# Placing the split of the last stage's weights, and the final norm's second broadcast, in a hybrid diffusion trunk layer

## The chip, the cores and the metric

The kernel runs on one core of one Trainium2 chip, written at the level of single engine instructions. The metric is the device time of one execution in microseconds; before the change the median of three runs is 3129.58 us (3123.66 to 3132.76).

TensorE multiplies, VectorE, ScalarE and GpSimd work element by element, and SyncE's queue issues all the DMAs that matter here. All matrix work is done in a split form: an fp32 operand x becomes a rounded part h (`wih`, `wph`, `hh`, ...) and the rest l = x - h (`wil`, `wpl`, `hl`, ...), and one product is three passes, h by h, h by l and l by h. ScalarE makes h (`hi`), VectorE makes l (`lo`).

## The reference

One trunk layer is evaluated for 2048 latent and 256 context tokens with shared weights (D_MODEL 1024, four branches of width 512):

```
h = rmsnorm(x) * (1 + scale) + shift
u = h @ w_in                                   # 8960 columns, split among the branches
o_att, o_conv, o_pool, o_ssm = the four mixers of the columns of u
br = [o_att*silu(g_att), o_conv*silu(g_conv), o_pool*silu(g_pool), o_ssm*silu(g_ssm)]
proj = einsum('blnw,nwd->blnd', br, w_br)      # each branch to 1024
merged = sum over branches of sigmoid(g_mrg) * proj
y = rmsnorm(x + gate * (merged @ w_out)) * final_g
```

The attention is a softmax over a band of latent keys, the context keys and a sink. The convolution has 31 taps per channel and a layer norm behind it. The scan branch ends in a product with `glu_w`. So `glu_w`, `w_br` and `w_out` are first needed near the end, and `w_in` all through.

## The kernel before

**Stages.** The tokens are six chunks of 384 columns, in three groups of 768. The first stage (to about 1065 us) makes the modulation, the normed h and the scan, with input columns of `w_in` beside it. The second (to about 2346 us) computes the other input columns, ten planner steps to each, while convolution, pooling and attention run in the background. The third takes each group through `glu_group` (the scan branch's last product), `merge_group` (32 products with `w_br`), `out_group` (8 products with `w_out`) and `last_norm`.

**Who orders the work.** `flow` writes out TensorE's order. It holds one dense stream (the columns) and a list of background streams, all of them Python generators. A generator yields what it waits for: tiles, a time of the planner's clock (a float), or a condition. The class `Clock` estimates when each tile is ready, and `flow` takes a background stream as soon as it is ready by that clock, and the dense stream otherwise; if nothing is ready it moves the clock forward. The order so found is binding for TensorE alone (`manual_schedule(engines={PE})`). On ScalarE, VectorE, GpSimd and SyncE a scheduler with a cost model of its own orders the instructions by when it believes their inputs and buffers to be ready; it may put an instruction before others that the program issued earlier. On the chip each of these engines takes its instructions in the order so fixed.

**The pieces.** `presplits` is a background stream of the second stage. It splits `glu_w`, `w_br` and `w_out` in 112 pieces of [128, 2, 128], with a load into a raw buffer `wps`, `hi` into `wph` on ScalarE, `lo` into `wpl` on VectorE and a store of each into a scratch tensor in HBM (`wd_glu`, `wd_br`, `wd_out`), from which the third stage fetches whole tiles. Piece n may be issued once `self.steps >= n * rate` with `rate = 0.9 * self.total / 112`, where `total` is the number of column steps of the stage. There are three buffers `wps`, with loads two pieces ahead, and one `wph` and one `wpl`.

**The tie.** `queue(eng, ins)` adds an ordering without a semaphore: `ins` may not be put before the instruction that was issued last on that engine when `self.behind` was taken. Before the change only the convolution's taps use it. `clock.last` holds each engine's latest instruction.

**The maxima.** `att_max` computes scores `mw` into PSUM, and VectorE adds the mask and takes the row maximum in one instruction (`tensor_tensor_reduce`), whose elementwise result goes into a scratch tile `junk` that nobody reads.

**The final norm.** `out_group` ends with `self.norms += 1` and hands `last_norm` over as a background stream. `last_norm` adds up the squares on TensorE (`st`), forms the reciprocal root, and then for each of two chunks m: VectorE builds a diagonal `dg`, TensorE broadcasts it with a product by ones into `rb` (one PSUM bank), VectorE multiplies eight tiles of the result with it, and they are stored. Between `dg` and the broadcast the stream holds for 4 us of the planner's clock in the first two groups (`g < 2`). At the end `self.norms -= 1`. The next group's `merge_group` computes its first column and then yields `(lambda: not self.norms,)`, and issues nothing more until that is true.

Of the kernel before, what the change touches and what calls it, by code (L numbers as in the profile page):

```python
# [12 lines left out]
F32 = mybir.dt.float32  # L13
F32R = mybir.dt.float32r
# [7 lines left out]
CH = 384  # L22
# [12 lines left out]
def f32(ap):  # L35
    return ap.bitcast(F32)
# [151 lines left out]
class K:  # L188
# [75 lines left out]
        return self.nc.sync.dma_start(out, in_)  # L264

    def hi(self, out, in_, scale=1.0):
        self.nc.scalar.activation(out, in_, AF.Copy, scale=scale)

    def lo(self, out, in_, hi, scale=None, eng=None):
        eng = eng or self.nc.vector  # L270
        if scale is None:
            eng.tensor_tensor(out, in_, f32(hi), op=OP.subtract)
        else:
            eng.scalar_tensor_tensor(out, in_, scale, f32(hi), op0=OP.mult, op1=OP.subtract)

    def rsqrt(self, pool, v, n, eng=None):
        V = eng or self.nc.vector
# [97 lines left out]
    def presplits(self, keys, pool):  # L375

        parts = [(key, k) for key in keys for k in range(0, self.WSRC[key[0]][1], 2)]
        rate = 0.9 * self.total / len(parts)
        got, to = [], {}

        def fetch(key, k):
            x = pool.tile([128, 2, 128], F32, name="wps", tag="wps", bufs=3)
            src = self.A[self.WSRC[key[0]][0]][key[1:] if len(key) > 2 else key[1]]
            self.load(x, src[:, k:k + 2])
            got.append(x)

        for p in parts[:2]:
            fetch(*p)
        for n, (key, k) in enumerate(parts):
            yield (lambda n=n: self.steps >= n * rate,)  # L390
            if n + 2 < len(parts):
                fetch(*parts[n + 2])
            kt = self.WSRC[key[0]][1]
            if k == 0:
                to[key] = self.dp.tile([2, 128, kt, 128], F32, name="wd_" + "_".join(str(x) for x in key))
            x = got.pop(0)
            h = pool.tile([128, 2, 128], F32R, name="wph", tag="wph", bufs=1)
            l = pool.tile([128, 2, 128], F32R, name="wpl", tag="wpl", bufs=1)
            self.hi(h, x)
            self.lo(l, x, h)  # L400
            for i, x in enumerate((h, l)):
                self.store(to[key][i][:, k:k + 2], f32(x))
            if k + 2 == kt:
                self.wcache[key] = to[key]
# [371 lines left out]
    def conv_setup(self, cp):  # L776
        nc, A = self.nc, self.A
        self.cw = cp.tile([128, 4, 31], F32, name="cw")
        self.cvec = cp.tile([128, 4, 4], F32, name="cvecs")
        self.load(self.cw, A["conv_dw"])  # L780
        self.load(self.cvec, A["conv_vec"])
        nc.vector.tensor_scalar(self.cw, self.cw, 0.5, None, op0=OP.mult)
        self.cgb = cp.tile([128, 4, 2], F32, name="cgb")
        nc.vector.tensor_scalar(self.cgb, self.cvec[:, :, 1:3], 0.5, None, op0=OP.mult)
        o5 = cp.tile([128, 128], F32R, name="o512")
        nc.vector.tensor_scalar(o5, self.ones, 1.0 / 512, None, op0=OP.mult)
        self.o512 = o5
        self.pwh = cp.tile([128, 4, 128], F32R, name="pwh")
        self.pwl = cp.tile([128, 4, 128], F32R, name="pwl")
        for k in range(0, 4, 2):  # L790
            x = cp.tile([128, 2, 128], F32, name="pw", tag="wps", bufs=3)
            self.load(x, A["pool_w"][:, k:k + 2])
            self.hi(self.pwh[:, k:k + 2], x)
            self.lo(self.pwl[:, k:k + 2], x, self.pwh[:, k:k + 2])
        self.pvec = cp.tile([128, 4], F32, name="pvec")
        self.load(self.pvec, A["pool_scale"])
        self.pfix = cp.tile([128, 4, 16], F32, name="pfix")
        self.load(self.pfix, A["pool_fix"])
# [34 lines left out]
    def queue(self, eng, ins):  # L833

        last = self.behind.get(eng)
        if last is not None:
            self.tc.add_manual_dep(ins.ins, last.ins.name, mybir.DependencyInfo(mybir.DependencyClass.NoSync,
                                                                               mybir.DependencyReason.DATA),
                                   reason="taps")

    def conv_taps(self, gc, mp, taps):

# [218 lines left out]
    def att_max(self, b, kv, t0, ka, kb, v, ap, st):  # L1061
# [32 lines left out]
        if wn:  # L1094
            for h in range(4):
                ps = self.px("mw", "m")[:, :wn]
                yield ps, ka
                nc.tensor.matmul(ps, qa[:, h, :], ka[:, w0:w0 + wn], start=True, stop=True)
                junk = ap.tile([128, CH], F32, name="junk", tag="junk", bufs=1)
                nc.vector.tensor_tensor_reduce(out=junk[:, :wn], in0=ps, in1=self.mask[:, moff:moff + wn], scale=1.0,  # L1100
                                               scalar=mc[:, h:h + 1], op0=OP.add, op1=OP.max,
                                               accum_out=mf[:, h:h + 1])

# [546 lines left out]
    def last_norm(self, g, y, S, mp, chunks):  # L1650

        nc = self.nc
        n = 3 * len(chunks)
        c0 = 3 * chunks[0]
        st = self.px("st", "x")
        Sf = S.rearrange("p c t -> p (c t)")
        yield Sf[:, c0 * 128:(c0 + n) * 128], st
        for i in range(n):
            nc.tensor.matmul(st[:, 2 * i:2 * i + 2], Sf[:, (c0 + i) * 128:(c0 + i + 1) * 128], self.ones[:, 0:2],
                             start=True, stop=True)  # L1660
        v = mp.tile([128, 6], F32, name="rms_v", tag="rms_v", bufs=2)
        nc.vector.tensor_scalar(v[:, :n], st[:, 0:2 * n].rearrange("p (i w) -> p i w", w=2)[:, :, 0], 1.0 / 1024, 1e-6,
                                op0=OP.mult, op1=OP.add)
        r = self.rsqrt(mp, v[:, :n], n, nc.gpsimd if g < 2 else None)
        sh = [128, 3, 128]
        for m, c in enumerate(chunks):
            dg = mp.tile(sh, F32, name="dg", tag="dg", bufs=1)
            nc.vector.tensor_tensor(dg, self.ident[:, None, :].to_broadcast(sh),
                                    r[:, 3 * m:3 * m + 3, None].to_broadcast(sh), op=OP.mult)
            rb = self.px("rb", "x")  # L1670
            yield dg, rb
            yield (self.clock.t + (4.0 if g < 2 else 0.0),)
            nc.tensor.matmul(rb[:, :CH], self.ones, dg.rearrange("p i q -> p (i q)"), start=True, stop=True)
            for d in range(8):
                yy = y[d][:, c * CH:(c + 1) * CH]
                nc.vector.scalar_tensor_tensor(yy, yy, self.fg[:, d:d + 1], rb[:, :CH], op0=OP.mult, op1=OP.mult)
                self.store(self.O["yT"][2 * g + c][:, d], yy)
        self.norms -= 1
# [302 lines left out]
```

## Time and profile before

| what | value |
|---|---|
| median of 3 runs | 3129.58 us (3123.66 to 3132.76) |
| profiled execution | 3132.41 us, its span 3130.7 us |
| TensorE matmuls | 2957.9 us, 94% of the span |
| VectorE | 2020.9 us, 65% |
| ScalarE | 1035.9 us, 33% |
| GpSimd | 874.4 us, 28% |
| mean granted clock of TensorE | 0.976 |
| DMA | 711.17 MB, mean 227 GB/s |

The profile records one execution. Busy times are per engine and may overlap; the granted clock is the share of full speed that TensorE was given, and 1.0 is 2.4 GHz. A matmul's end is modelled, so a busy share tells that TensorE had work, not that it ran at its peak. Nearly every instruction goes through one helper line (L162), so the rows are told apart by their tiles: `mm` is a bank of column products, `pj` of branch products, `tg`, `sg`, `mge`, `px`, `qf` are evictions of columns.

### The profile page before, as it was taken

To read this page: it belongs to the slowest core of one execution; us is meant where nothing else is said; L and a number is where in the kernel's file an instruction comes from. 1 tells how busy PE (TensorE), PEld (TensorE's weight loads), DVE (VectorE), ACT (ScalarE), POOL (GpSimd) and SP (SyncE) were. 2 spreads that over 40 slices of the span, in tenths; PEclk is the share of its full clock that TensorE was granted. 3 is DMA by queue.
4 is the path that set the end of the run, shared out by engine and by line. 5 is a ranking of instruction groups with operands and counts; after the bars stand their busy time and mean duration, and the time that the engine had idled before them with its cause. 6 is when DMAs were issued, how large, how long until landed. Compare 5 with 4: busy or idle time off the path is not lost.

```text
span 3130.7 us, 46156 instructions
## 1 busy us (share of the span) xinstructions
PE 2957.9 (94%) x16316; PEld 2823.2 (90%) x16316; DVE 2020.9 (65%) x3525; ACT 1035.9 (33%) x2029; POOL 874.4 (28%) x1124
## 2 busy tenths in 40 slices
PE   8979998999999998989999999999999999999998
PEld 4978898999899997989888889999999999999998
DVE  6835787767687476778787677777313653653663
ACT  5522333332332243335454444454312011011011
POOL 0953352434343131442232333233100001001001
PEclk9989999999999998999999999999999999999999
DMA  9665556565665688887767656575578976976967
GB/s 365 205 220 207 211 184 216 196 224 196 241 223 174 196 279 277 266 245 209 225 205 225 199 152 173 166 243 154 159 222 283 321 227 226 340 247 222 327 198 243
DMA packets 379904, 711.17 MB, mean 227 GB/s; under 512 B 83513, under 2 KB 207257, under 8 KB 378393
## 3 DMA queue, kind: packets, MB, share of 16 engines
q1 hardware_dynamic: 379672, 708.22, 68.9%
q8 instruction: 129, 2.11, 0.3%
q14 instruction: 103, 0.84, 0.1%
HBM read 470.43 MB, written 229.83 MB: 224 GB/s over the span
## 4 chain that ended last, share of the span: by engine, by line
PE 37%; DMA 7%; DVE 5%; issue 1%; ACT 1%; SPq 1%; DVEq 0%; ACTq 0%
PE mm L162 20%; PE pj L162 12%; PE ov L162 2%; DVE acc L162 2%; PE sT L162 1%; DMA bs<-sg_d 1%; DMA wbh<-wd_br 1%; DMA wd_out<-wpl 1%; DMA wd_out<-wph 1%; SPq L162 1%; DMA wil<-wd_out 1%; DMA bo<-o_d 0%; PE mw L162 0%; DVE wpl L162 0%; DVE pl L162 0%
## 5 line engine op out<-in xcount | busy, mean ns | idle before, releaser
L162 PE MATMUL mm<-hh,wih 128*128 128x384 f32 x3840 | 801.9, 343 | 67.8 <-ACT tg L162 28.1
L162 PE MATMUL mm<-hh,wil 128*128 128x384 f32 x3840 | 784.7, 338 | 8.1 <-DVE wil L162 8.1
L162 PE MATMUL mm<-hl,wih 128*128 128x384 f32 x3840 | 789.3, 339 | 1.2 <-DMA hl<-h_d 1.2
L162 PEld LDWEIGHTS mm<-hh,wih 128*128 128x128 f32 x3840 | 688.2, 192 | 89.5 <-ACT tg L162 32.1
L162 PEld LDWEIGHTS mm<-hl,wih 128*128 128x128 f32 x3840 | 688.2, 191 | 8.5 <-issue 3.1
L162 PEld LDWEIGHTS mm<-hh,wil 128*128 128x128 f32 x3840 | 683.5, 190 | 12.8 <-DVE wil L162 9.5
L162 DVE SCALAR_TENSOR_TENSOR acc<-cbuf,cw,acc 128x384 f32<-128x384 f32 (+1 forms) x540 | 412.9, 770 | 7.3
L162 POOL TENSOR_TENSOR acc<-acc,cprod 128x384 f32<-128x384 f32 (+1 forms) x180 | 218.1, 1212 | 359.6 <-ACT cprod L162 353.6
L162 PE MATMUL pj<-hh,wbh 128*128 128x384 f32 x768 | 167.6, 341 | 1.6 <-DMA wbh<-wd_br 1.6
L162 PE MATMUL pj<-hh,wbl 128*128 128x384 f32 x768 | 165.6, 338 | 0.0
L162 PE MATMUL pj<-hl,wbh 128*128 128x384 f32 x768 | 165.6, 338 | 0.0
L162 DVE TENSOR_TENSOR wil<-wis,wih 128x1024 fp32r<-128x1024 f32 x68 | 88.5, 1301 | 112.9 <-ACT wih L162 88.7
L162 ACT ACTIVATE mge<-mm 128x384 f32<-128x384 f32 x192 | 91.9, 484 | 207.1 <-PE mm L162 202.4
L162 POOL TENSOR_TENSOR oS<-oS,osq 128x384 f32<-128x384 f32 x36 | 37.9, 1054 | 419.4 <-ACT osq L162 419.4
L162 DVE TENSOR_TENSOR pl<-p,ph 128x512 fp32r<-128x512 f32 x164 | 125.1, 769 | 30.0 <-ACT ph L162 29.9
L162 ACT ACTIVATE wih<-wis 128x1024 fp32r<-128x1024 f32 x68 | 72.2, 1061 | 217.1 <-DMA wis<-w_in 138.4
L162 PEld LDWEIGHTS pj<-hh,wbh 128*128 128x128 f32 x768 | 137.6, 190 | 4.2 <-issue 4.2
L162 PEld LDWEIGHTS pj<-hh,wbl 128*128 128x128 f32 x768 | 137.1, 190 | 0.0
L162 PEld LDWEIGHTS pj<-hl,wbh 128*128 128x128 f32 x768 | 137.1, 190 | 0.0
L162 DVE TENSOR_TENSOR wpl<-wps,wph 128x256 fp32r<-128x256 f32 x112 | 59.0, 527 | 116.0 <-ACT wph L162 38.7
L162 ACT ACTIVATE hh<-bo 128x768 fp32r<-128x768 f32 x48 | 38.9, 841 | 276.9 <-PE pj L162 163.4
L162 DVE SCALAR_TENSOR_TENSOR mt<-mt,pj 128x384 f32<-128x384 f32 x144 | 79.4, 551 | 68.0 <-PE pj L162 62.4
(416 smaller groups left out, 4186.4 us busy)
## 6 DMA issues: line engine op xcount, KB each, us to landing
wih<-wd_in SPq DMA_DIRECT2D x132, 512.0 KB
wil<-wd_in SPq DMA_DIRECT2D x132, 512.0 KB
mg_d<-mge SPq DMA_DIRECT2D x96, 384.0 KB
mt<-mg_d SPq DMA_DIRECT2D x96, 384.0 KB
wis<-w_in SPq DMA_DIRECT2D x70, 512.0 KB
wd_in<-wih SPq DMA_DIRECT2D x66, 512.0 KB
wd_in<-wil SPq DMA_DIRECT2D x66, 512.0 KB
wbh<-wd_br SPq DMA_DIRECT2D x96, 256.0 KB
```

Of the source, the lines that this page charges most:

```text
L162: r = f(*args, **kw)
```

## The change

`hi` and `lo` now return their instruction, so that `presplits` can tie both behind the engine's latest work. The raw buffers become two and loads run one piece ahead; the rounded parts get two buffers each. The maxima write their elementwise result back over the scores in PSUM, and the scratch tile is gone. The second broadcast of the final norm is held 10 us instead of 4 in the first two groups.

```diff
     def hi(self, out, in_, scale=1.0):
-        self.nc.scalar.activation(out, in_, AF.Copy, scale=scale)
+        return self.nc.scalar.activation(out, in_, AF.Copy, scale=scale)
...
         def fetch(key, k):
-            x = pool.tile([128, 2, 128], F32, name="wps", tag="wps", bufs=3)
+            x = pool.tile([128, 2, 128], F32, name="wps", tag="wps", bufs=2)
...
-        for p in parts[:2]:
-            fetch(*p)
+        fetch(*parts[0])
         for n, (key, k) in enumerate(parts):
             yield (lambda n=n: self.steps >= n * rate,)
-            if n + 2 < len(parts):
-                fetch(*parts[n + 2])
+            if n + 1 < len(parts):
+                fetch(*parts[n + 1])
...
-            h = pool.tile([128, 2, 128], F32R, name="wph", tag="wph", bufs=1)
-            l = pool.tile([128, 2, 128], F32R, name="wpl", tag="wpl", bufs=1)
-            self.hi(h, x)
-            self.lo(l, x, h)
+            h = pool.tile([128, 2, 128], F32R, name="wph", tag="wph", bufs=2)
+            l = pool.tile([128, 2, 128], F32R, name="wpl", tag="wpl", bufs=2)
+            self.behind = dict(self.clock.last)
+            self.queue("scalar", self.hi(h, x))
+            self.queue("vector", self.lo(l, x, h))
...
-            x = cp.tile([128, 2, 128], F32, name="pw", tag="wps", bufs=3)
+            x = cp.tile([128, 2, 128], F32, name="pw", tag="wps", bufs=2)
...
-                junk = ap.tile([128, CH], F32, name="junk", tag="junk", bufs=1)
-                nc.vector.tensor_tensor_reduce(out=junk[:, :wn], in0=ps, in1=self.mask[:, moff:moff + wn], scale=1.0,
+                nc.vector.tensor_tensor_reduce(out=ps[:, 0:wn], in0=ps, in1=self.mask[:, moff:moff + wn], scale=1.0,
                                                scalar=mc[:, h:h + 1], op0=OP.add, op1=OP.max,
                                                accum_out=mf[:, h:h + 1])
...
-            yield (self.clock.t + (4.0 if g < 2 else 0.0),)
+            yield (self.clock.t + (4.0 + 6.0 * m if g < 2 else 0.0),)
```

## Rows read from the trace of the kernel before

**Rows 1.** Windows of 200 us: length, busy per engine (instructions), clock, DMA share, GB/s
```profile
1000.00:1200.00 200.00, 189.59 (x1079) 182.13 (x1078) 132.09 (x238) 71.93 (x160) 49.37 (x56) 0.98 0.70 226
1200.00:1400.00 200.00, 169.94 (x901) 164.21 (x900) 138.12 (x229) 66.63 (x139) 75.00 (x62) 0.92 0.87 273
1400.00:1600.00 200.00, 186.37 (x980) 174.48 (x980) 159.66 (x304) 105.28 (x232) 53.45 (x51) 0.96 0.69 211
1600.00:1800.00 200.00, 188.19 (x988) 173.19 (x987) 150.12 (x291) 95.36 (x207) 56.52 (x57) 0.98 0.68 212
1800.00:2000.00 200.00, 196.45 (x1051) 184.56 (x1050) 153.74 (x274) 98.27 (x196) 66.47 (x64) 0.98 0.57 165
2000.00:2200.00 200.00, 197.28 (x1073) 185.75 (x1072) 154.12 (x286) 97.63 (x192) 64.24 (x62) 1.00 0.60 190
```

**Rows 2.** Windows of the second stage, instructions of tile wph alone (VectorE, ScalarE)
```profile
1077.00:1400.00 323.00, 28.01 (x52) 21.74 (x53) 0.94 0.85 270
1400.00:1800.00 400.00, 30.97 (x60) 25.00 (x60) 0.97 0.68 212
1800.00:2210.00 410.00, 0.00 (x0) 0.00 (x0) 0.99 0.58 177
```

**Rows 3.** Tile wph: durations, first and last start; waits before it; waits for it
```profile
L162 ACT ACTIVATE wph<-wps x112: 399/418/426, 1080.1 to 1790.1; 128x256 fp32r<-128x256 f32 x112
...
  DMA wd_br<-wph: 78.6, 31
...
  ACT wph L162: 157.3, 69
```

**Rows 4.** Windows of the second stage, instructions of tile mm alone (PE first)
```profile
1077.00:1400.00 323.00, 268.57 (x1410) 255.82 (x1409) 0.00 (x0) 37.74 (x84) 0.94 0.85 270
1400.00:1800.00 400.00, 272.63 (x1407) 253.30 (x1408) 0.00 (x0) 39.34 (x89) 0.97 0.68 212
1800.00:2210.00 410.00, 290.13 (x1537) 269.86 (x1536) 0.00 (x0) 31.62 (x65) 0.99 0.58 177
2210.00:2330.00 120.00, 110.90 (x626) 108.54 (x625) 0.00 (x0) 12.74 (x26) 1.00 0.61 194
```

**Rows 5.** Timeline, TensorE waits with a piece in front: start, length, instruction [idle before <-releaser]
```profile
1172.41 1.68 PE L162 MATMUL mm<-hh,wih 128*128 128x384 f32 x8 [1.34 <-ACT tg L162]
...
1356.83 0.42 ACT L162 ACTIVATE wph<-wps 128x256 fp32r<-128x256 f32 x1 [3.35 <-DVE wpl L162]
1357.68 1.65 PE L162 MATMUL mm<-hh,wih 128*128 128x384 f32 x4 [5.08 <-ACT tg L162]
...
1755.51 0.80 PE L162 MATMUL sT<-qa,ka 128*128 128x512 f32 x1 [2.85 <-ACT p L162]
```

**Rows 6.** Whom TensorE waited for: us in total, times, longest
```profile
PE mm L162 <- ACT tg L162: 28.1, 12, 5.4
```

**Rows 7.** Timeline, TensorE waits with a piece beside another late item, first and last
```profile
1202.48 1.66 PE L162 MATMUL mm<-hh,wih 128*128 128x384 f32 x8 [1.75 <-ACT tg L162]
...
1537.63 0.27 PE L162 MATMUL mT<-ident,mf 128*4 128x128 f32 x1 [2.13 <-DVE mf L162]
```

**Rows 8.** Groups of VectorE instructions: shapes, count, busy us, mean ns, idle before
```profile
L162 DVE TENSOR_TENSOR merged<-merged,mt 128x384 f32<-128x384 f32 x144 | 83.7, 581 | 3.1
L162 DVE SCALAR_TENSOR_TENSOR mt<-mt,pj 128x384 f32<-128x384 f32 x144 | 79.4, 551 | 68.0 <-PE pj L162 62.4 <-DMA mt<-mg_d 3.6 <-DMA wbl<-wd_br 0.9
L162 DVE CUSTOM_DVE_ANT_0 junk<-mw,mask,mc 128x384 f32<-128x384 f32 (+1 forms) x128 | 75.5, 590 | 15.6 <-PE mw L162 12.9
```

**Rows 9.** Timeline of the first group's two broadcasts
```profile
2661.29 0.81 PE L162 MATMUL rb<-dg,ones 128*128 128x384 f32 x2
...
2666.95 1.65 PE L162 MATMUL rb<-dg,ones 128*128 128x384 f32 x2 [4.85 <-DVE dg L162]
```

**Rows 10.** Window behind the second broadcast, columns as in rows 1
```profile
2668.00:2672.00 4.00, 4.00 (x13) 3.70 (x13) 4.00 (x8) 0.64 (x1) 0.00 (x0) 0.50 1.07 398
```

**Rows 11.** Whom SyncE's queue waited for: us in total, times, longest
```profile
SPq L162 <- PE mm L162: 376.5, 182, 14.9
```

More of the change, by code (lines that the diff above doesn't have):

```diff
@@ L271, in lo @@
         if scale is None:
-            eng.tensor_tensor(out, in_, f32(hi), op=OP.subtract)
+            return eng.tensor_tensor(out, in_, f32(hi), op=OP.subtract)
         else:
-            eng.scalar_tensor_tensor(out, in_, scale, f32(hi), op0=OP.mult, op1=OP.subtract)
+            return eng.scalar_tensor_tensor(out, in_, scale, f32(hi), op0=OP.mult, op1=OP.subtract)
     def rsqrt(self, pool, v, n, eng=None):
@@ L838, in queue @@
                                                                                mybir.DependencyReason.DATA),
-                                   reason="taps")
+                                   reason="step")
     def conv_taps(self, gc, mp, taps):
```

## The prediction

> **What bounds the kernel now.** I read the windows of 200 us first, then who TensorE waited for, then the tiles that the diff touches, then the order in time around single waits. The reader should see in the windows [rows 1] that TensorE sets the time: between 1800 and 2200 us it is busy 196.45 and 197.28 of 200 us, so little can be won there. From 1000 to 1800 us it is not: it idles 10.4, 30.1, 13.6 and 11.8 us (200 less its busy time), 65.9 us in all, at a mean granted clock of 0.98, 0.92, 0.96 and 0.98. A clock of 0.92 means that part of the time was spent at the 1.2 GHz level instead of 2.4; I price it as (1 - clock) x 200 us, so 4 + 16 + 8 + 4 = 32 us. The same two sums for 1800 to 2200 are 6.3 and 4 us. Both stretches belong to one stage (input projection, with convolution, pooling and attention beside it), and what differs beside the mix of columns is the weight pieces of `presplits`.
>
> The count of pieces in the same stretches says so: 53 ScalarE roundings from 1077 to 1400, 60 from 1400 to 1800 and none after [rows 2], the last at 1790.1 us [rows 3]. The code asks for something else. Piece n may start once n x 0.9/112 of the stage's column steps are done. Steps can be counted by the column matmuls, ten steps to 48 of them: 1410, 1407, 1537 and 626 up to 2330 us [rows 4], about 90 more to the end of the stage, some 5070. A piece every 0.9 x 5070/112 = 41 matmuls would give 35 pieces by 1400, 34 from 1400 to 1800, and 43 from there to about 2250. So the pieces ran ahead of their place: nothing in the program of before ties them, and the order on ScalarE, VectorE and SyncE is made by a scheduler that takes what it believes ready.
>
> Running ahead, each piece meets the one before. There is one `wph` and one `wpl`, and ScalarE's rounding had to wait for the slot in 69 cases, 157.3 us; the part put down to the stores into `wd_br` alone is 78.6 us in 31 waits [rows 3]. ScalarE has slack for that, but an eviction queued behind the waiting piece has not: at 1356.83 a `wph` had waited 3.35 us for VectorE's `wpl`, the eviction `tg` came right behind it, and TensorE, with two banks for columns, stood 5.08 us [rows 5]. That is the largest of twelve waits of `mm` for `tg` [rows 6].
>
> **The change part by part.** The sum is made against the profiled execution: span 3130.7 us, 3132.41 us with what lies around it, 2.8 us above the median of the three runs (3129.58).
>
> *Waits that go.* I went through TensorE's waits of over 1.3 us between 1060 and 1800 and looked at what ScalarE or VectorE did just before each. Eight have a piece's own wait directly in front of the eviction or reduction that TensorE needed: 1.34, 2.96, 1.71, 3.07, 5.08, 1.51, 2.08 and 2.85 us, together 20.6 (the first, the largest and the last are [rows 5]). Four more (1.75, 1.95, 2.14, 2.13 us, first and last in [rows 7]) have a piece beside another late item; I count half, 4.0. With the tie a piece stands no earlier than the work issued last, some 8 to 11 us after the one before, and with two rounded buffers it needs the store of the piece before that, so these waits should go: -24.6 us. The rest of the 65.9 us (the reload of `hh`, late queries, maxima late on VectorE) has no piece in it and stays.
>
> *The clock that comes back.* 24.6 of 65.9 us of idle time is 37%. I take the same share of the 32 us: -12 us. From below it could be nothing, if the short waits never moved the clock; from above all 32.
>
> *What the moved pieces cost.* Each moved piece brings its ScalarE rounding, VectorE subtraction, one load and two stores on SyncE. 43 of them come into 1800 to 2250, where TensorE now idles 6.3 us in 400. Between nothing (each hidden under columns, ScalarE being busy 98 of 200 us there, [rows 1]) and the old price per piece, (24.6 + 12)/112 = 0.33 us, they cost 0 to 14 us; late stragglers among the other 69 come on top. I take +6. The bytes are the same; only their place changes, which relieves 1077 to 1400.
>
> *One load ahead instead of two*, and three raw buffers become two. A load has one piece interval, 323/35 = 9 us early and 450/43 = 10 us late, to land. What is queued behind a piece whose load is late is every eviction on ScalarE. I cost it at nothing, hidden by that interval; if the cover fails it is the second rival. The pool weights use the same two buffers once, at the start of the stage; nothing.
>
> *The maxima write into PSUM instead of `junk`.* No row shows VectorE writing PSUM. The nearest: a fused op that reads PSUM takes 551 ns, an add with SBUF operands alone 581, the masked maximum itself 590 [rows 8]. So +-0.04 us on each of 128, +-5 us of VectorE time, and TensorE sees a part of it at most, since VectorE has slack (154 of 200 us busy, [rows 1]). I take 0, by the 551 row, where the operand in PSUM costs nothing more. The Trainium skill speaks against it: "Perfetto Trace Analysis", section "Optimizing Scalar/DVE Operations", puts VectorE's fixed access at about 60 ns on SBUF and 125 on PSUM. As an estimate that is 65 ns x 128 = 8 us of VectorE, and if all of it reached TensorE the sum would be 8 us smaller. The rows disagree on the reading side, and no row shows the writing side. The planner also sees the four maxima of a block finish sooner, because they no longer share one buffer, so it may put transposes a little earlier on TensorE; its sign is open, I take 0 and let the waits of over 2 us that I left out above, a few of them on maxima, bound it at +-5 us.
>
> *The second broadcast 6 us later* (groups 0 and 1). The wait is real: 4.85 us of TensorE [rows 9], and the 4 us behind it run at 0.50, the 1.2 GHz level [rows 10], which gives away 2 more; 6.9 us twice is 13.7 us. But look at what TensorE did between the two broadcasts: nothing. The code already holds the second one 4 us, and a planner that could place matmuls there would have. It could not: the next group's first merge column waits until the norm is over (`not self.norms`), and the first broadcast stands exactly at that column's end. Holding the second longer moves only the planner's own clock. I take 0; the bounds are 0 and -13.7.
>
> Sum: -24.6 - 12 + 6 + 0 + 0 + 0 = -30.6 us. 3132.4 - 30.6 = 3101.8, and 2.8 less for the median: **3099 us**.
>
> **The rivals.**
>
> *The waits pass to the next in the queue.* Behind a piece there is often another item that the scheduler put too early (the pooling's rounding, the layer norm's). Then TensorE's waits keep their number and the sum shrinks to about the clock of two or three long waits, 2 us each: 3125 us. For it: of TensorE's large waits some have only such an item in front. Against it: the quiet stretch from 1800 has all those items too, and loses a fifth as much (10.3 us in 400 against 97.9 in 800).
>
> *The load is late, and the kernel gets slower.* SyncE takes its queue in order, and one hold until column matmuls had let go of a buffer lasted 14.9 us [rows 11], longer than the 9 to 10 us a load now has. A tied rounding then waits on ScalarE in front of evictions, where before two loads were under way. The Trainium skill states the rule it would go by: in "PSUM — Partial Sum Buffer", section "Engine vs sequencer instructions", the queues of ScalarE, VectorE and GpSimd are strict FIFO; the trace agrees at 1356.83. Price: before, 157.3 us of piece waits came with 36.6 us of TensorE loss, 0.23 each. If the 112 pieces wait more than 1.4 us on average for their loads, the gain is gone; at 2.5 us each, 280 us x 0.23 = 65, so 3132 + 65 - 37 - 3 = 3157 us. Against it: holds of 14.9 us are the longest of 182, whose mean is 2.1.
>
> *The tie moves nothing.* If the scheduler can still take pieces early, because the latest work on an engine is itself early, only the second pair of buffers counts; half of the 24.6 us goes and no clock: 3117 us.
>
> *The second broadcast does get filled*, on top of the forecast: 3099 - 13.7 = 3085 us.
>
> **How the numbers follow.** The forecast gets 0.55, the filled broadcast 0.05, the tie that moves nothing 0.10 (0.08 faster, 0.02 the same), the passed-on waits 0.17, the late load 0.13. A change of 0.3%, 9.4 us, is about what a measurement of this kernel can tell from none. Faster (below 3120): 0.55 + 0.05 + 0.08 = 0.68; same 0.02 + 0.17 = 0.19; slower 0.13. The likeliest case's own range is 3072 (1000 to 1800 us nearly as quiet as 1800 to 2200: 97.9 us of loss less 20.6 at the quiet rate and 20 that has no piece in it, 57 us) to 3119 (only the eight waits and no clock, 14 us for the moved pieces, 5 for the planner). The range for 8 in 10 takes in the passed-on waits and a little of the late load: 3070 to 3134.
>
> **What would show it.** Right: pieces at about 35, 34 and 43 in the three stretches, the last near 2250; `wph` slot waits far below 157 us; `mm` for `tg` well under 28.1 us [rows 6]; the clock of 1200 to 1400 at 0.95 or more; the second broadcast still 4.85 us late in both groups. Wrong: roundings waiting on their loads; the same waits of TensorE under other names; pieces still ending near 1790; or new idle time from 1800 to 2250 of over 14 us.

## The result, and the profile after

The changed kernel takes 3086.28 us (median of four runs, 3083.82 to 3088.67) against 3126.62 us (3122.75 to 3132.76) for the kernel before: a ratio of 0.9868, with a 95% interval of 0.9852 to 0.9885. That is 40 us; the forecast was 30.6 us and 3099 us. The profiled executions differ by more, 3132.41 against 3086.06 us, because that of before lay 5.8 us above its median and that of after at its median.

**Where the time came from.** The first eviction of the third stage (`gt`) starts at 2389.2 us before and at 2339.5 after. These windows are cut there. First the kernel before; columns as in [rows 1].

```profile
0.00:1000.00 1000.00, 926.01 (x5128) 864.34 (x5129) 704.52 (x1188) 350.40 (x647) 431.64 (x687) 0.97 0.64 221
...
2200.00:2389.20 189.20, 187.46 (x1064) 184.55 (x1063) 38.69 (x66) 45.51 (x85) 12.58 (x14) 1.00 0.62 194
2389.20:3130.70 741.50, 716.59 (x4068) 710.02 (x4066) 389.87 (x656) 104.90 (x175) 65.10 (x72) 0.98 0.80 266
```

The same cut of the kernel after:

```profile
0.00:1000.00 1000.00, 928.14 (x5128) 866.97 (x5128) 704.27 (x1188) 350.98 (x647) 431.93 (x687) 0.97 0.64 221
...
2200.00:2339.50 139.50, 138.34 (x799) 137.75 (x798) 17.17 (x37) 25.12 (x48) 3.48 (x4) 1.00 0.70 221
2339.50:3084.30 744.80, 716.71 (x4068) 710.74 (x4066) 388.52 (x656) 105.30 (x175) 65.14 (x72) 0.98 0.79 265
```

And the six windows of 200 us that answer to [rows 1], after:

```profile
1000.00:1200.00 200.00, 193.86 (x1114) 186.35 (x1113) 140.45 (x239) 73.35 (x162) 52.63 (x57) 0.99 0.69 225
1200.00:1400.00 200.00, 175.95 (x952) 171.83 (x953) 141.69 (x230) 66.65 (x138) 72.46 (x62) 0.93 0.79 256
1400.00:1600.00 200.00, 194.49 (x1053) 182.65 (x1052) 175.70 (x332) 112.49 (x243) 58.57 (x58) 0.99 0.66 206
1600.00:1800.00 200.00, 198.87 (x1084) 188.06 (x1083) 158.10 (x293) 103.15 (x212) 65.98 (x63) 1.00 0.67 206
1800.00:2000.00 200.00, 198.38 (x1082) 187.66 (x1081) 155.79 (x292) 103.24 (x212) 60.72 (x63) 1.00 0.67 206
2000.00:2200.00 200.00, 196.64 (x1050) 184.59 (x1049) 146.10 (x262) 96.96 (x198) 57.78 (x58) 0.98 0.68 210
```

The reader should see the whole account in these. Up to `gt` TensorE starts 12,250 matmuls in both kernels (a matmul that lies across the edge of two windows is in the x of both, so that the first column adds up to a few more: 12,264 before, 12,262 after). Its idle time there (window less busy time) falls from 147.9 to 114.8 us, by 33.1: 2.1 of it in the first 1000 us, 29.1 from 1000 to 1800 (65.9 to 36.8), 1.9 later. Its busy time for these same matmuls falls from 2241.3 to 2224.7, by 16.6: they ran at the higher clock for longer. Together 49.7 us, all ahead of the third stage, which itself became 3.3 us longer (741.5 to 744.8). 46.4 us remain, the difference of the two spans. These are single executions. A second profile of a program with the same order on every engine as the kernel before (the later broadcast alone, below) has 143.5 us of idle time and 2240.0 us of busy time up to its `gt`, 5.7 us less in sum than here.

**The pieces.** The windows of [rows 2], of tile `wph` alone (VectorE, ScalarE), after:

```profile
1077.00:1400.00 323.00, 19.52 (x37) 15.40 (x38) 0.95 0.79 259
1400.00:1800.00 400.00, 18.77 (x37) 14.47 (x36) 1.00 0.67 206
1800.00:2250.00 450.00, 17.96 (x38) 15.26 (x38) 0.99 0.67 209
```

And what answers to [rows 3]: the roundings, the waits before them, and who waited for them.

```profile
L162 ACT ACTIVATE wph<-wps x112: 400/404/430, 1086.6 to 2201.2; 128x256 fp32r<-128x256 f32 x112
...
  ACT wph L162: 25.4, 10
  DMA wps<-w_br: 16.0, 6
...
  DVE wpl L162: 25.4, 10
```

The rows `ACT wph` and `DVE wpl` of 25.4 us are one thing seen from two sides: VectorE's subtraction waiting for the rounding. 38, 36 and 38 roundings where there were 53, 60 and none; the last at 2201 us instead of 1790. No rounding waits for a slot any more (157.3 us before); there are 18.9 us of waits for loads in their place (16.0 for `w_br`, 2.9 for `glu_w`).

**Whom TensorE waited for from 1000 to 1800 us** (us in total, times, longest). Before, the row of `tg` and the two largest that name the maxima:

```profile
PE mm L162 <- ACT tg L162: 12.3, 6, 5.1
PE mT L162 <- DVE mf L162: 7.6, 4, 3.3
PE mw L162 <- DVE mf L162: 7.3, 4, 4.6
```

After, the largest rows of all:

```profile
PE mx L162 <- POOL acc L162: 8.5, 1, 8.5
PE mm L162 <- ACT tg L162: 7.6, 7, 2.8
...
PE mm L162 <- ACT px L162: 5.2, 1, 5.2
...
PE mT L162 <- DVE mf L162: 2.3, 4, 0.9
PE mw L162 <- DVE mf L162: 1.4, 1, 1.4
```

The waits for the gate's eviction `tg` fell from 12.3 to 7.6 us there (28.1 to 21.3 in the whole program, [rows 6]). More came from the attention's maxima: all rows that name `mf` or `mc` make 20.7 us before and 6.2 after. Two single waits of 8.5 and 5.2 us are more than a third of the 36.8 that is left; before, the largest for the same tiles were 2.7 (`mx`) and 3.1 us (`px`). Both have a piece ahead of them, on the queue that the tie does not touch, SyncE's. The one of 5.2 us ends at 1291.53 with the eviction `px`, which stands on ScalarE behind `qh`, and `qh` behind the loads `qs<-qf`. Their input was done at 1273.96, but SyncE stood from 1273.93 to 1277.54, 3.6 us, at the store of a `wpl` that VectorE finished at 1277.51:

```profile
1277.54 0.32 SPq L162 DMA_DIRECT2D wd_br<-wpl  x1
...
1279.41 2.45 SPq L162 DMA_DIRECT2D qs<-qf  x4
```

The one of 8.5 us ends at 1371.91 with the first `mx`, which needs the queries `qa`. The profile names GpSimd's `acc`, but that was done at 1367.10; the load of `qa` was issued only at 1367.59, behind another store that SyncE held until VectorE's `wpl` ended at 1365.04:

```profile
1365.06 0.32 SPq L162 DMA_DIRECT2D wd_br<-wpl  x1
...
1367.59 1.58 SPq L162 DMA_DIRECT2D qa<-qk_d  x2
```

In the 25 us before the first load of `qa` SyncE issues 8 loads and stores of pieces in the kernel before and 12 in the kernel after. This is read from the traces; no run puts the pieces' loads and stores elsewhere.

**The second broadcast** (start, length, instruction, idle before it) in the first group, after, and the masked maxima, which answer to [rows 9] and [rows 8]:

```profile
2611.44 0.81 PE L162 MATMUL rb<-dg,ones 128*128 128x384 f32 x2
2617.09 1.65 PE L162 MATMUL rb<-dg,ones 128*128 128x384 f32 x2 [4.85 <-DVE dg L162]
```

```profile
L162 DVE CUSTOM_DVE_ANT_0 mw<-mw,mask,mc 128x384 f32<-128x384 f32 (+1 forms) x128 | 74.1, 601 | 12.3 <-PE mw L162 12.0
```

The wait is 4.85 us as before. A maximum written to PSUM takes 601 ns, against 590 to `junk`; it reads its scores from PSUM in both.

### The profile page after: what moved, and what is told of

The parts are those of the page before. It is cut to its first block, busy times and chain, and to the rows that moved or that the text cites. A ratio compares the mean times of both kernels' runs of the same rounds, so it can differ in the third digit from the quotient of the medians.

```text
span 3084.3 us, 46115 instructions
## 1 busy us (share of the span) xinstructions
PE 2941.4 (95%) x16316; PEld 2816.6 (91%) x16316; DVE 2027.8 (66%) x3525; ACT 1037.2 (34%) x2029; POOL 868.7 (28%) x1124
## 4 chain that ended last, share of the span: by engine, by line
PE 57%; DVE 18%; DMA 12%; POOL 5%; issue 3%; ACT 2%; SPq 2%; DVEq 0%; POOLq 0%; ACTq 0%
PE mm L162 36%; PE pj L162 12%; DVE acc L162 3%; PE ov L162 3%; DMA wis<-w_in 3%; SPq L162 2%; PE sT L162 2%; DVE w L162 1%; DVE wil L162 1%; POOL sp_t L162 1%; DVE vr L162 1%; DVE wr L162 1%; DMA hl<-h_d 1%; DVE wi L162 1%; PE mps L162 1%
## 5 line engine op out<-in xcount | busy, mean ns | idle before, releaser
L162 PE MATMUL mm<-hh,wih 128*128 128x384 f32 x3840 | 798.6, 341 | 56.9 <-ACT tg L162 21.3
L162 PEld LDWEIGHTS mm<-hh,wih 128*128 128x128 f32 x3840 | 684.4, 191 | 77.3 <-ACT tg L162 25.7
L162 PEld LDWEIGHTS mm<-hl,wih 128*128 128x128 f32 x3840 | 688.3, 191 | 12.1 <-DMA hl<-h_d 5.9
L162 DVE SCALAR_TENSOR_TENSOR acc<-cbuf,cw,acc 128x384 f32<-128x384 f32 (+1 forms) x540 | 427.8, 794 | 8.0
L162 ACT ACTIVATE ph<-p 128x512 fp32r<-128x512 f32 x164 | 100.3, 632 | 58.6 <-POOL p L162 57.5
```

The costliest lines, as they stand in the source:

```text
L162: r = f(*args, **kw)
```

## Experiments

Each was timed beside the kernel before on the same chip, and the ratio is to that. The theory: the tie brings the gain, since it makes the pieces stand apart. The first rivals: the second pair of buffers alone; the maxima; the later broadcast.

**The tie alone**, put into the kernel before; one `wph`, one `wpl`, three raw buffers, the maxima into `junk`.

```diff
...
-            self.hi(h, x)
-            self.lo(l, x, h)
+            self.behind = dict(self.clock.last)
+            self.queue("scalar", self.hi(h, x))
+            self.queue("vector", self.lo(l, x, h))
```

> The kernel before with the tie alone: three raw buffers and two loads ahead, one wph, one wpl, junk and the 4 us hold stay. The planner's order on TensorE stays that of before. Theory (the tie is the change, because pieces then stand apart): the pieces spread to about 2200 us, the slot waits of wph (157.3 us before) fall below 40 us, and the ratio to before is 0.987 to 0.990, nearly all of the 0.9868. Rival A (the second pair of buffers is what counts): ratio 0.995 or more, with slot waits still over 100 us. Rival B (the other order on TensorE that the planner found is what counts): ratio 0.997 to 1.003 whatever the slot waits do.

3092.38 us (3088.24 to 3102.14), 0.9891 [0.9876, 0.9907]. TensorE's instructions stand in the order that they have in the kernel before. The pieces are 36, 38 and 38, the last at 2218.7 us. TensorE idles 45.7 us from 1000 to 1800 (65.9 before, 36.8 with the whole change). The roundings, and three rows of TensorE's waits from 1000 to 1800:

```profile
L162 ACT ACTIVATE wph<-wps x112: 398/410/422, 1089.3 to 2218.7; 128x256 fp32r<-128x256 f32 x112
...
PE mm L162 <- ACT tg L162: 5.0, 5, 2.3
...
PE mw L162 <- DVE mc L162: 2.5, 4, 1.6
PE mw L162 <- DVE mf L162: 1.8, 2, 1.3
```

`tg` is down to 5.0 and the maxima to 6.0 (from 12.3 and 20.7), with `junk` still there. So the tie alone gives 35 of some 40 us, and the waits fall behind ScalarE and VectorE both; tying on one engine alone was not tried. One number missed: the roundings still waited 54.2 us for their slot, where under 40 was expected, and TensorE did not suffer from it.

**Everything but the tie**: the kernel after with the two plain calls put back.

```diff
-            self.behind = dict(self.clock.last)
-            self.queue("scalar", self.hi(h, x))
-            self.queue("vector", self.lo(l, x, h))
+            self.hi(h, x)
+            self.lo(l, x, h)
```

> The changed kernel without the tie: two wph, two wpl, two raw buffers, maxima into PSUM, the 10 us hold stay. Theory (the tie): pieces run ahead again, the last before 1900 us; ratio to before 0.995 to 1.003. Rival A (the buffers): ratio 0.990 or less. Rival B (the planner's order on TensorE, which is that of the changed kernel here): ratio 0.990 or less, also with pieces that end early.

3102.55 us (3099.12 to 3106.2), 0.9930 [0.9917, 0.9942]. Neither expectation holds as it stood: the rest of the change does bring something, more than the theory gave it and less than the rivals did. The pieces run further ahead than before (windows of `wph`, then two of the waits before the roundings):

```profile
1077.00:1400.00 323.00, 36.99 (x66) 27.25 (x66) 0.95 0.89 289
1400.00:1800.00 400.00, 22.07 (x46) 19.17 (x46) 0.98 0.68 209
1800.00:2250.00 450.00, 0.00 (x0) 0.00 (x0) 1.00 0.58 176
```

```profile
  DMA wps<-w_br: 83.2, 40
...
  DMA wps<-w_out: 35.4, 20
```

With a second pair the slot holds nobody; the loads do, 118.6 us in these two rows and 8.0 more for `glu_w`. TensorE's order is that of the kernel after, so the step from here to that kernel is the tie's alone: 16 us by the medians (3086.28), 19 by the ratios (0.9868). The parts do not add up: the tie gives 35 us by itself, the rest without it 22, both together 41 by the ratios, since both take away some of the same waits.

**The maxima into PSUM alone**, in the kernel before:

```diff
-                junk = ap.tile([128, CH], F32, name="junk", tag="junk", bufs=1)
-                nc.vector.tensor_tensor_reduce(out=junk[:, :wn], ...
+                nc.vector.tensor_tensor_reduce(out=ps[:, 0:wn], ...
```

> The kernel before with the maxima written over the scores in PSUM alone. Theory: the masked maximum takes 590 ns as before within 20 ns, and the ratio is 0.998 to 1.002, what is left being the planner's other order on TensorE. Rival (the write into PSUM costs the fixed access more): the maximum takes 650 ns or more and the ratio is 1.001 to 1.004. Rival B (the order counts): ratio 0.990 or less.

3120.62 us (3108.14 to 3124.63, eleven runs), 0.9968 [0.9954, 0.9982]: a small gain, a little outside what the theory allowed. The pieces end at 1785.5 us and TensorE's waits for maxima are 24.5 us, so it does none of what the tie does. But without the shared `junk` the planner has another order for TensorE. The next run makes the same edit and holds that order fixed:

```diff
...
+            if method == "tensor_tensor_reduce":
+                start = max(start, self.held)
             end = self.place(eng, start, fixed + size * each)
+            if method == "tensor_tensor_reduce":
+                self.held = end + self.SEEN
```

> The kernel before with the maxima written into PSUM, and the planner told that they still follow one another as if they shared a buffer, so that TensorE's order is that of before, instruction by instruction (VectorE, ScalarE and SyncE are ordered anew by the scheduler). Theory (the 0.9968 of the maxima alone came from the planner's other order on TensorE): 0.999 to 1.001. Rival (it came from the write itself, or from the other engines' order): 0.996 to 0.998 again.

3124.52 us (3117.78 to 3131.31, twelve runs), 0.9988 [0.9977, 0.9999], with TensorE's order that of the kernel before. The two intervals overlap by a little; that most of the 0.3% is the order is likely, not shown.

**The tie and the maxima, without second buffers** (the two diffs above; one `wph`, one `wpl`, three raw buffers, the old hold).

> The kernel before with the tie and the maxima into PSUM, but one wph, one wpl and three raw buffers as before. Theory (beside the tie the second pair of buffers adds little, and the rest of the step from 0.9891 to 0.9868 is the planner's other order on TensorE): 0.9865 to 0.988. Rival (the buffers give that rest): 0.989 or more, with slot waits of wph near the tie's alone.

3082.14 us (3080.71 to 3086.3), 0.9855 [0.9832, 0.9877]: as fast as the whole change. The wait of its roundings for their slot:

```profile
  ACT wph L162: 69.2, 25
```

So the second pair adds nothing that can be told once the pieces stand apart, and a slot wait as such need not cost anything: 69.2 us of them here beside 38.3 us of idle time of TensorE from 1000 to 1800, 36.8 in the kernel after. Against the maxima without the tie (0.9968, the same order on TensorE) the tie is worth 35 us by the ratios.

**The later broadcast alone**, in the kernel before:

```diff
-            yield (self.clock.t + (4.0 if g < 2 else 0.0),)
+            yield (self.clock.t + (4.0 + 6.0 * m if g < 2 else 0.0),)
```

> The kernel before with the second broadcast's hold of 10 us alone. Theory: the order on every engine is that of before, instruction by instruction, both waits of 4.85 us stay, and the ratio is 1.000 within its interval; it shows what this measurement makes of no change. Rival (the hold is filled): the waits go and the ratio is 0.9955.

3127.16 us (eleven runs), 1.0003 [0.9993, 1.0012]. Every engine has the same order, and both waits stand (the second broadcast of the first and of the second group):

```profile
2659.87 1.39 PE L162 MATMUL rb<-dg,ones 128*128 128x384 f32 x2 [4.85 <-DVE dg L162]
```

```profile
2905.55 1.31 PE L162 MATMUL rb<-dg,ones 128*128 128x384 f32 x2 [4.85 <-DVE dg L162]
```

**Letting merge columns in ahead of the second broadcast.** The prediction blamed the gate in front of the next group's first merge column. Here it stands at the third column; in the next run at the fourth, with 11 `merged` and 3 `mt` buffers.

```diff
                 if i == 0:
-                    yield (lambda: not self.norms,)
+                    if d == 2:
+                        yield (lambda: not self.norms,)
```

> The changed kernel with merge_group's wait for the norm moved from its first column to its third, so that the planner may put up to two columns (18 matmuls of some 0.174 us, 3.1 us) between the two broadcasts. Theory (the gate, not the hold, kept the second broadcast next to the first): the two waits of 4.85 us shrink to 1.7 us or so each, the clock behind them stays at 1.0, and the time falls by 6 to 12 us against the changed kernel (some 0.9868 to 0.984 of before). Rival (the wait is VectorE's chain of eight products and nothing hides it): no change, since the two columns' own evictions queue on VectorE behind those products and TensorE stands a little later.

3089.02 us (3084.39 to 3090.22), 0.9872 [0.9852, 0.9892]: nothing over the kernel after. First group, the second broadcast and the merge column behind it (4.31 and 2.36 us in the second group):

```profile
2622.12 0.91 PE L162 MATMUL rb<-dg,ones 128*128 128x384 f32 x2 [2.26 <-DVE dg L162]
...
2632.74 1.01 PE L162 MATMUL pj<-hh,wbh 128*128 128x384 f32 x4 [3.97 <-DVE merged L162]
```

> The changed kernel with that wait at the fourth column, eleven merged buffers instead of ten and three gate buffers mt instead of four to make room. Thirty matmuls, 5.2 us, then stand between the broadcasts. Theory: both waits go altogether and the time falls by 10 to 14 us against the changed kernel, 0.983 of before. Rival: the columns run out of pj banks, as VectorE does the eight products of the norm first, and the wait appears at the columns instead, no more than 3 us won in all; or the three mt buffers cost new waits of pj evictions on their loads.

3081.32 us (3073.68 to 3088.19), 0.9852 [0.9829, 0.9876]. The broadcasts wait no more, the columns do (the first group's two; 2.82 and 4.49 us in the second), and what VectorE does before the later of them:

```profile
2611.91 0.97 PE L162 MATMUL pj<-hh,wbh 128*128 128x384 f32 x4 [1.48 <-DVE merged L162]
...
2624.40 1.95 DVE L162 SCALAR_TENSOR_TENSOR merged<-mt,pj 128x384 f32<-128x384 f32 x4 [5.17 <-DMA o_yT<-merged]
2625.01 1.65 PE L162 MATMUL pj<-hh,wbh 128*128 128x384 f32 x4 [5.94 <-DVE merged L162]
```

From the first `gt` to the end this kernel takes 744.7 us, the kernel after 744.8, so its lower median is not the gate's. The theory falls: filling the gap moves TensorE's wait to the columns, as the rival says, and VectorE has no wait for the loads of `mt`. But the rival's cause, VectorE's eight products, is only the first part of it. VectorE is through with them at 2619.23 and then stands 5.17 us (3.71 in the second group) until the stores of the result have freed a `merged` buffer for the next column.

**The pieces at their old pace.** The kernel after with the pieces let go earlier, so that they end near 1790 us, tie and buffers kept.

```diff
-        rate = 0.9 * self.total / len(parts)
+        rate = 0.55 * self.total / len(parts)
```

> The changed kernel with the pieces issued over 0.55 of the stage's steps instead of 0.9, so that they end near 1750 us as they did before, tied all the same. Theory A (what counts is that a piece stands behind the latest work, wherever it is): 0.985 to 0.990 of before, as the changed kernel. Theory B (what counts is that they are spread thin, 34 per 400 us instead of 60): 0.992 to 0.996, with the loss in 1077 to 1800 us back and 1800 to 2200 quiet.

3118.38 us (3114.32 to 3128.68, twelve runs), 0.9972 [0.9959, 0.9985]: most of the gain is gone, more than any theory had allowed. The pieces are 59, 53 and 0, TensorE's idle time from 1000 to 1800 is 69.3 us again, and its two largest waits in that stretch are

```profile
1387.66 1.19 PE L162 MATMUL mx<-kca,qa 128*128 128x256 f32 x4 [13.82 <-DMA qb<-qk_d]
```

```profile
1447.49 0.71 PE L162 MATMUL mean<-lnh,o 128*128 128x414 f32 x1 [7.79 <-ACT lnh L162]
```

The waits for maxima stay low (8.4 us). The pace also changes the planner's order on TensorE, so the time by itself doesn't tell bunched pieces from an unlucky order. The trace shows pieces ahead of both waits. In the 25 us before the load of `qa` SyncE issues 23 loads and stores of pieces, 12 in the kernel after, and one store holds it 2.6 us for a `wpl`. In front of `lnh` ScalarE takes two roundings that start 2.5 us after their loads were issued. With these late loads the wait of the prediction's second rival comes back: the roundings wait 79.3 us for loads, 18.9 in the kernel after. The two waits are 21.6 of the 69.3 us; the rest was not traced. A pace between, 0.72, which changes the order as much:

```diff
-        rate = 0.9 * self.total / len(parts)
+        rate = 0.72 * self.total / len(parts)
```

> The changed kernel with the pieces issued over 0.72 of the steps, between e7's 0.55 and the change's 0.9; they should end near 1980 us. If the spread is what counts, the time lies between, 0.990 to 0.994 of before; if e7's loss was one unlucky order (its single wait of 13.8 us), 0.986 to 0.989.

3084.59 us (3081.92 to 3089.82), 0.9868 [0.9852, 0.9884]: no loss, with 46, 47 and 19 pieces, the last at 1968.7 us. The roundings wait 40.0 us for loads, SyncE issues 15 loads and stores of pieces in the 25 us before `qa`, and the wait there is 8.84 us. So the loss is not in proportion to the bunching. Whether it sets in somewhere between 46 and 59 early pieces, and how much of it is the order's, stays open; the early pace with two loads ahead was not run.

**Two loads ahead again**: the kernel after with three raw buffers.

```diff
-            x = pool.tile([128, 2, 128], F32, name="wps", tag="wps", bufs=2)
+            x = pool.tile([128, 2, 128], F32, name="wps", tag="wps", bufs=3)
...
-        fetch(*parts[0])
+        for p in parts[:2]:
+            fetch(*p)
...
-            if n + 1 < len(parts):
-                fetch(*parts[n + 1])
+            if n + 2 < len(parts):
+                fetch(*parts[n + 2])
...
```

> The changed kernel with three raw buffers and loads two pieces ahead again. Theory (a load has a piece interval of 10 us and lands in time, so depth there is worth nothing): 0.985 to 0.989, the 16.0 us of ScalarE's waits for loads gone without a gain on TensorE. Rival (loads one ahead cost part of the gain): 0.984 or less.

3081.86 us (3077.06 to 3086.78), 0.9858 [0.9841, 0.9874]. The roundings' waits for loads are gone; the interval lies across that of the kernel after. One load ahead costs nothing that can be told.

**The norm's products taken off VectorE.** On the kernel with the tie and the maxima: in groups 0 and 1 both `dg` are made first, ScalarE copies each broadcast out of PSUM, and every second product goes to ScalarE (the scale) and GpSimd (the product).

```diff
...
+            s = rb[:, :CH]
+            if g < 2:
+                s = S[:, c]
+                nc.scalar.activation(s, rb[:, :CH], AF.Copy)
             for d in range(8):
                 yy = y[d][:, c * CH:(c + 1) * CH]
-                nc.vector.scalar_tensor_tensor(yy, yy, self.fg[:, d:d + 1], rb[:, :CH], op0=OP.mult, op1=OP.mult)
+                if g < 2 and d % 2:
+                    nc.scalar.activation(yy, yy, AF.Copy, scale=self.fg[:, d:d + 1])
+                    nc.gpsimd.tensor_tensor(yy, yy, s, op=OP.mult)
+                else:
+                    nc.vector.scalar_tensor_tensor(yy, yy, self.fg[:, d:d + 1], s, op0=OP.mult, op1=OP.mult)
```

> The tie and the PSUM maxima (as e8), and in groups 0 and 1 both diagonals built first, the broadcast copied out of PSUM by ScalarE, and every second product of the norm taken off VectorE (scale on ScalarE, product on GpSimd); the gate stays at the first column. Theory after e5 and e6 (VectorE's sixteen products are what the two broadcasts and the columns behind them wait for): the second broadcast waits under 1.5 us, the merge columns behind it under 2 us in sum, the clock stays up, and the time falls by 8 to 14 us against e8, to 0.981 to 0.983 of before. Rival (GpSimd's eight products, 8 to 10 us, and the merged buffers they hold are the next wait): no gain, 0.985 to 0.987.

3075.36 us (3074.0 to 3076.6), 0.9836 [0.9821, 0.9851]: the lowest median of all, though its interval overlaps that of the kernel that it was built on (0.9832 to 0.9877) and ends just below that of the kernel after (0.9852 to 0.9885). TensorE's order is that of the kernel that it was built on. The first group's second broadcast, and the column that waits now:

```profile
2608.79 0.91 PE L162 MATMUL rb<-dg,ones 128*128 128x384 f32 x2 [0.58 <-ACT oS L162]
```

```profile
2621.57 0.97 PE L162 MATMUL pj<-hh,wbh 128*128 128x384 f32 x4 [3.54 <-DVE merged L162]
```

4.85 us became 0.58 in each group; 3.54 came back at a merge column in each, where under 2 in sum was expected. From the first `gt` to the end it takes 736.7 us against 742.6 in the kernel that it was built on, 5.9 less; the medians, taken on different chips, differ by 6.8, a little under the 8 to 14 expected.

The theory's reason does not hold. VectorE's products of the norm, first in the kernel that this one was built on (all three groups), then here (groups 0 and 1, which read ScalarE's copy `oS`):

```profile
L162 DVE SCALAR_TENSOR_TENSOR merged<-merged,fg,rb 128x384 f32<-128x384 f32 x48 | 25.7, 609 | 4.0 <-PE rb L162 3.8
```

```profile
L162 DVE SCALAR_TENSOR_TENSOR merged<-merged,fg,oS 128x384 f32<-128x384 f32 x16 | 19.6, 1282 | 1.2 <-ACT oS L162 1.2
```

Sixteen products take 19.6 us here, where the 32 of groups 0 and 1 took some 17 (two thirds of 25.7). Beside GpSimd's products, 1337 ns each, those of VectorE take some 1370 ns instead of 609; the one in the first group that starts after GpSimd's last takes 606. So VectorE was not relieved. By the trace it is the rest of the edit that closed the gap: the second diagonal no longer stands behind eight products, and ScalarE's copy frees the bank of the first broadcast at once; it is the copy that the second broadcast now waits for. The rival came true in part: GpSimd's eight products take 10.4 us, VectorE's stretch with them, and the merge additions behind them are late by the 3.54 us. The diagonals and the copy without moving products were not run.

## Why the prediction was right, and where it was off

The mechanism holds: tied pieces spread out, ScalarE and VectorE stop being late, and TensorE gets back idle time and clock. The tie alone shows it, with the rest of the program and TensorE's order as before. The size was 10 us short, by these steps:

- *Waits that go*, -24.6 us: right in sign, too small. TensorE idled 29.1 us less from 1000 to 1800 and 33.1 less up to the third stage. The list of what would stay was wrong in one point, "maxima late on VectorE": those waits fell by 14.5 us, and in the run of the tie alone by as much, so the pieces had a part in making them late. The prediction looked only at what stood directly in front of a wait; that a piece further up VectorE's queue counts too is likely, not shown. The waits for `tg`, its largest example, fell by 6.8 us only, so "well under 28.1" was missed. That sign was set on the wrong row: 28.1 us is the whole program's, of which 12.3 lie from 1000 to 1800, and its longest wait of 5.4 us is at 310 us, long before the first piece; the 5.08 is the largest of the second stage only.
- *The clock*, -12 us: the same matmuls took 16.6 us less busy time; by the prediction's own way of pricing, (1 - clock) x 200, 32 us became 18 from 1000 to 1800. The share of idle time was the right key here, 44% of both, and came out larger with it. From 1200 to 1400 the clock is 0.93 and not 0.95 or more: this window has the two single waits of 8.5 and 5.2 us.
- *What the moved pieces cost*, +6 us: looked for in the wrong place. From 1800 to 2200 TensorE idles 5.0 us with the pieces there, 6.3 without, at the same clock cost of 4 us. The old price of a piece does not carry over to pieces that stand apart there. But the pieces that now stand ahead of the queries' load on SyncE have a part in the wait for `mx`, 8.5 us instead of 2.7.
- *The planner's order*, 0 +- 5: likely a gain of a few us. The tie with the maxima takes 10 us less than the tie alone, on another chip; their intervals, 0.9832 to 0.9877 and 0.9876 to 0.9907, only touch. With the order held the maxima by themselves leave 0.9988 [0.9977, 0.9999].
- *One load ahead*, 0: right. *The second pair of buffers*, which the prediction gave a part in the waits: wrong for the tied pieces, which do as well with one pair.
- *The maxima into PSUM*, 0: right in the durations, 11 ns more each. The Trainium skill's rule in "Perfetto Trace Analysis", section "Optimizing Scalar/DVE Operations", would have had some 65 ns as an estimate, if it holds for the output alone; the trace does not agree with that.
- *The second broadcast*, 0: right, and shown with the same order on every engine. The reason given, that the next group's gate keeps work out, explains the order, but not the price: of the rival at 3085 us nothing could be had through the gate, since the merge additions were the next to be late.

The late load did come, at 18.9 us in seven waits, an eighth of the 157 us that would have used up the gain (112 pieces at 1.4 us). The tie does move the pieces. As far as the traces were followed, the waits passed on in one place, to the loads behind the pieces' stores on SyncE's queue.

The range has a slip. Its slow end of 3119 us does not follow from its terms: the eight waits' 20.6 us less 14 for the moved pieces and 5 for the planner leave a gain of 1.6, 3128 us. The time of 3086 lies nearer the fast end, 3072, whose terms fit.

The third stage's 3.3 us were in no step. It idles 28.1 us instead of 24.9; TensorE's waits for third-stage weights (`pj` for `wbh` and `wbl`) are 4.3 us there instead of 1.6, and for `merged` 1.7 instead of 0.4. Little of it can be told from chance: the run of the later broadcast alone, with every engine's order as before, takes 738.9 us there, 2.6 less than the kernel before, and waits 3.2 us for `wbh`.

## What to carry to other kernels

Background work that a scheduler may take early should be tied to its place, on each engine whose queue it shares with urgent work; its count by stretch in the trace says whether it runs ahead. The queue of loads and stores is such a queue too: here a piece's store held SyncE 3.6 us in front of an urgent load. Judge its waits by what TensorE loses: 69 us of waits for a slot cost nothing that could be told where the pieces stood apart. Before filling a gap on the engine that sets the time, see what is late next: here it was a buffer that a store had to free. And after moving work off an engine, read the durations of what stays: VectorE's products took twice as long beside GpSimd's, and by the trace the gap closed through the order of the diagonals and the early copy.

## What the runs showed that was not expected

- Where work stands moves such a kernel more than how much there is: the two programs with the tie and single buffers differ by 10 us (3082.14 and 3092.38, the maxima's place and TensorE's order), two paces of the same pieces by 34 (3084.59 and 3118.38).
- The second stage does not run alike from one execution to the next: the first `gt` stands at 2339.5 us in the profile of the kernel after, at 2340.0 with the gate at the third column and at 2327.3 with it at the fourth, which share the code up to there. The last is the fastest of five executions of its program, which lie 14.5 us apart. Its idle time up to `gt` is that of the kernel after (114.9 and 114.8 us); the same matmuls took 12.1 us less, so the difference is the clock's. A gain in the third stage is therefore better read from `gt` to the end than from the whole time.
- The same wait does not cost the same clock each time: behind 4.85 us of idle time the second broadcast's two matmuls take 1.65 us in the kernel after and 1.39 and 1.31 with the later broadcast alone; behind 2.26 and 0.58 us they take 0.91. The first broadcast's, in the midst of work, take 0.81.
